# A hybrid encoder layer on one NeuronCore: the products and sums of its state space branch on VectorE, attention's tables through GpSimd's queue, one transfer where there were four

## The chip, the core and the metric

The kernel runs on one NeuronCore of a Trainium2 chip. The engines that appear below are TensorE (PE in the rows, and PEld for its weight loads), VectorE (DVE), ScalarE (ACT), GpSimd (POOL) and SyncE (SP), whose queue issues most of the transfers. The metric is device time in microseconds (us), the median of the runs: the kernel before takes 1432.58 us (three runs, 1430.61 to 1438.53).

## The reference

One layer of an encoder on 1024 tokens (a grid of 16 rows by 64 columns) of width 1024, all in float32. Three branches read the same projection and are merged through gates; a feed-forward part follows.

```python
h = rms_norm(x, g_mix);  z = h @ w_in          # Fourier 256 | q, k, v 3 x 512 | S5 input 256 | gates 3 x 1024
A = real(fftn(positions, group channels))      # 4 groups of 64 channels
B = neighbourhood_attention(q, k, v, rpb)      # 8 heads of 64, window 8 rows x 16 columns, a bias per head
# C: 16 groups of 16 channels, 64 complex states, both directions
lam_bar = exp(lam * dt);  bu = einsum('bsgc,gpc->bsgp', u, b_bar)
xs = associative_scan(x[t] = lam_bar * x[t-1] + bu[t])         # forward, and reversed
y = d_skip * u + sum over directions of real(einsum('bsgp,gcp->bsgc', xs, c))
y = gelu(y);  C = y * sigmoid(y @ w_glu)
merged = sum_i sigmoid(gate_i) * (branch_i @ w_br_i);  x = x + merged @ w_out
x = x + relu(rms_norm(x) @ w_up)**2 @ w_down;  out = rms_norm(x)
```

## The kernel before, in words

Activations lie transposed, channels on the 128 partitions, in two halves of 512 tokens. A float32 product is made of three matmuls on values split into a high and a low part: ScalarE writes the high part (`split`, line 196; `w_cut`, line 142) and VectorE subtracts it for the low one (lines 197, 143). The long projections run in `mm_main`, whose matmuls are line 171; they are called the main matmuls here, and every third of them makes a tick.

At each tick the branches, written as Python generators, may go on by a step. A branch has a rate (0.4 steps a tick for the state space branch, 0.57 for attention, 0.5 for the Fourier branch), and each `yield` in it ends a step. So a `yield` more puts what follows it behind two or three more ticks of main matmuls, and TensorE's instructions, in program order, are main matmuls with the branches' small ones between them. The other engines get their instructions in the order in which the Tile scheduler, with a timeline of its own, puts them; an engine works through its order and waits at an instruction whose inputs are not there.

The state space branch (`ssm`) treats its 16 groups in four quarters of four groups. `ssm_params` makes the exponentials and the powers pa, and bhat and bbar. Then three generators take turns. `ssm_prep` makes a quarter's matrices: `product` multiplies complex numbers of shape 128 x 512 into AA and BB, with some of the six multiplications and sums on GpSimd (G) and the rest on VectorE (V); line 464 transposes BB on TensorE, line 465 copies the result to BT on ScalarE; lines 454 and 455 put bbar into bz on GpSimd; line 469 multiplies bz by AA; kp and M come from that, M through eight transfers. `ssm_data` multiplies BT by U (line 501), turns the result by E (505 to 511), runs four scans on VectorE (515, 517), turns back (523 to 530), multiplies with M and AA (line 535) and writes Y to the scratch y_scr with four transfers. `ssm_gelu` reads yT back for every two quarters, once it is written, and computes GELU: Square on ScalarE (line 555), a product on VectorE (557), Tanh on ScalarE (559), a product on VectorE (561). At the end comes the GLU, whose weights glw are loaded at line 599.

Attention (`attn_pair`) runs over four pairs of heads, 16 units a pair: scores on TensorE (line 761), bias and maximum on VectorE (764, in the order's rows ISA), Exp on ScalarE (771), scaling by the reciprocal on VectorE or ScalarE (781, 779), transposes on TensorE (789), the split into p (196, 197), values on TensorE (806, 810), and the sum of two parts (819). Each unit loads a table bm of 192 KB four units ahead, and each two units a tile vj of 256 KB in four transfers of 64 KB out of the scratch v_scr. `attn_in` prepares q and k of the next pair (lines 722 to 730).

The first 40 us normalise the input, 40 to 100 us compute v, and up to 680 us run the gates' logits, the four pairs, the state space branch and the Fourier branch's start beside one another. After that come the merge (683 to 817 us) and the feed-forward part, where lines 165 and 1379 work.

Tiles come from pools with a set number of buffers: 36 of 4 KB (s), 21 of 2 KB (m) and 8 banks of PSUM. Who takes a buffer waits until its last reader is done.

## Time and profile before

| | |
|---|---|
| median of 3 runs | 1432.58 us (1430.61 to 1438.53) |
| profiled execution | 1433.98 us, of which the span of the trace is 1432.2 us |
| TensorE busy | 1383.5 us, 97% of the span |
| VectorE busy | 947.0 us |
| ScalarE busy | 572.0 us |
| GpSimd busy | 188.8 us |
| the chain that ended last | 83% of the span on TensorE, 7% on VectorE, 2% on transfers |

A row of a timeline gives the start, the duration, the engine, the line of the kernel, the operation with what it writes and reads, and in brackets how long the engine had been idle and who ended that. Consecutive instructions of an engine overlap a little at their ends, so the distance between two starts is what an instruction costs its engine. A row of the view by stretches gives each engine's busy time in a stretch, and behind that the mean clock that TensorE was granted (1.00 is 2.4 GHz, 0.50 is 1.2 GHz).

### The profile page before, as it was taken

The page shows a single profiled execution, that of the slowest core. Times are in us where ns is not written, and L with a number is a line of the kernel's source. Part 1 is how long each engine was busy: PE and PEld are TensorE (multiplying, and loading weights), DVE is VectorE, ACT ScalarE, POOL GpSimd, SP SyncE. Part 2 cuts the span into 40 slices and gives each one's busy share as a digit, 9 for nine tenths or more (in the row PEclk, how much of TensorE's full clock was granted, in tenths as well). Part 3 has the DMA queues.
Part 4 walks back from the last instruction along what each step waited for, and adds up shares of the span by engine and source line. Part 5 has one row for each costly group of instructions (what it writes and reads, how often), then busy time and mean ns, then how long its engine had stood idle before and what let it go on. Part 6 is the DMA issues. An engine that isn't in the chain of part 4 may idle for free.

```text
span 1432.2 us, 18648 instructions
## 1 busy us (share of the span) xinstructions
PE 1383.5 (97%) x6520; PEld 1152.1 (80%) x6520; DVE 947.0 (66%) x1764; ACT 572.0 (40%) x1087; POOL 188.8 (13%) x313
## 2 busy tenths in 40 slices
PE   6999988999999999999999999999999999999997
PEld 5778877788888888888788878888888788888885
DVE  6759876576473312543524797777777999878766
ACT  5512264566562211032401674333323364444244
POOL 3758611000000000000000003112211100000000
PEclk9999999999999999999999999999999999999998
DMA  6332453737563217411343226444447885454303
GB/s 227 136 121 82 132 165 99 215 111 239 170 215 127 99 42 255 145 43 35 96 162 114 78 89 213 140 154 148 143 155 265 278 298 176 147 175 143 96 8 117
DMA packets 110926, 209.62 MB, mean 146 GB/s; under 512 B 13681, under 2 KB 46833, under 8 KB 110833
## 3 DMA queue, kind: packets, MB, share of 16 engines
q1 hardware_dynamic: 100160, 174.09, 37.6%
q0 software_dynamic: 10672, 34.35, 6.5%
q8 instruction: 51, 0.84, 0.2%
q14 instruction: 43, 0.34, 0.1%
HBM read 146.52 MB, written 56.62 MB: 142 GB/s over the span
## 4 chain that ended last, share of the span: by engine, by line
PE 83%; DVE 7%; DMA 2%; issue 2%; ACT 1%; POOL 1%; SPq 1%; DVEq 0%; ACTq 0%; POOLq 0%
PE ps L165 45%; PE ps L171 34%; PE ps L789 1%; PE ps L806 1%; PE ps L810 1%; SPq L111 1%; DVE z L515 1%; DVE z L517 1%; DVE wl L143 0%; DMA vj<-v_scr 0%; PE ps L1083 0%; DMA bm<-in_rpb 0%; DVE BB L431 0%; DMA wr<-in_w_in 0%; DVE sm L764 0%
## 5 line engine op out<-in xcount | busy, mean ns | idle before, releaser
L165 PE MATMUL ps<-dw,dh 128*128 128x512 f32 x1344 | 306.1, 389 | 2.3 <-DVE dw L197 2.3
L165 PE MATMUL ps<-fb,uw 128*128 128x512 f32 x1344 | 306.6, 389 | 1.4 <-DVE t L1142 1.0
L165 PEld LDWEIGHTS ps<-dw,dh 128*128 128x128 f32 x1344 | 252.0, 188 | 55.7 <-DVE dw L197 3.2
L165 PEld LDWEIGHTS ps<-fb,uw 128*128 128x128 f32 x1344 | 251.9, 188 | 54.5 <-PE ps L1083 1.2
L171 PE MATMUL ps<-hTh,wh 128*128 128x512 f32 x576 | 231.7, 403 | 6.3 <-DVE mx L764 2.0
L171 PE MATMUL ps<-hTl,wh 128*128 128x512 f32 x576 | 227.6, 395 | 1.1 <-DVE hTl L200 1.1
L171 PE MATMUL ps<-hTh,wl 128*128 128x512 f32 x576 | 226.9, 394 | 0.0
L171 PEld LDWEIGHTS ps<-hTh,wh 128*128 128x128 f32 x576 | 109.3, 190 | 28.0 <-ACT wh L142 2.4
L171 PEld LDWEIGHTS ps<-hTh,wl 128*128 128x128 f32 x576 | 109.0, 189 | 22.9
L171 PEld LDWEIGHTS ps<-hTl,wh 128*128 128x128 f32 x576 | 109.5, 190 | 21.2 <-DVE hTl L200 1.5
L143 DVE TENSOR_TENSOR wl<-wr,wh 128x1024 fp32r<-128x1024 f32 (+2 forms) x76 | 72.5, 966 | 55.3 <-ACT wh L142 52.3
L196 ACT CAST dh<-da 128x512 fp32r<-128x512 f32 x112 | 69.5, 620 | 95.4 <-PE ps L165 61.2
L1379 DVE TENSOR_TENSOR x<-x,ps 128x512 f32<-128x512 f32 x112 | 73.6, 684 | 34.4 <-PE ps L165 34.3
L1295 POOL DMA_DIRECT2D h_scr<-hx x48 | 26.0, 541 | 493.7 <-ACT hx L1265 376.1
L197 DVE TENSOR_TENSOR dh<-da,dh 128x512 fp32r<-128x512 f32 x112 | 77.1, 688 | 13.8 <-ACT dh L196 13.8
L171 PE MATMUL ps<-act,wh 128*128 128x512 f32 x256 | 78.7, 390 | 0.1
L142 ACT CAST wh<-wr 128x1024 fp32r<-128x1024 f32 (+2 forms) x76 | 60.7, 821 | 32.1 <-PE ps L171 7.7
L196 ACT CAST uw<-us 128x512 fp32r<-128x512 f32 x64 | 38.1, 626 | 84.2 <-DVE us L1222 84.2
L1017 ACT ACTIVATE tg<-ps 128x512 f32<-128x512 f32 x32 | 19.1, 597 | 124.0 <-PE ps L171 118.6
L1267 DVE SCALAR_TENSOR_TENSOR hx<-hx 128x512 f32<-128x512 f32 x52 | 35.8, 689 | 40.7 <-ACT hx L1259 40.3
L764 DVE CUSTOM_DVE_ANT_0 sm<-ps,bm 128x384 f32<-128x384 f32 x64 | 35.3, 553 | 34.2 <-PE ps L165 24.2
L196 ACT CAST dw<-wd 128x512 fp32r<-128x512 f32 x80 | 49.4, 618 | 19.1 <-PE ps L165 18.4
(286 smaller groups left out, 2116.6 us busy)
## 6 DMA issues: line engine op xcount, KB each, us to landing
da<-h_scr SPq DMA_DIRECT2D x112, 256.0 KB
wr<-in_w_in SPq DMA_DIRECT2D x36, 512.0 KB
wu<-in_w_up SPq DMA_DIRECT2D x32, 512.0 KB
h_scr<-hs POOLq DMA_DIRECT2D x64, 256.0 KB, 2.6
wd<-in_w_down SPq DMA_DIRECT2D x64, 256.0 KB
bm<-in_rpb SPq DMA_DIRECT2D x64, 192.0 KB
h_scr<-hx POOLq DMA_DIRECT2D x48, 256.0 KB, 2.8
vj<-v_scr SPq DMA_DIRECT2D x128, 64.0 KB
```

The lines of the kernel that those rows point to most:

```text
L111: return self.nc.sync.dma_start(out=out, in_=in_)
L142: self.nc.scalar.copy(hi, r)
L143: self.nc.vector.tensor_tensor(out=lo, in0=r, in1=hi.bitcast(F32), op=ALU.subtract)
L165: self.nc.tensor.matmul(out=out, lhsT=l, rhs=r, start=start and i == 0, stop=stop and i == last, skip_group_check=more)
L171: self.nc.tensor.matmul(out=out, lhsT=l, rhs=r, start=i == 0, stop=i == last)
L196: nc.scalar.copy(hi, src)
L197: nc.vector.tensor_tensor(out=lo, in0=src, in1=hi.bitcast(F32), op=ALU.subtract)
L764: V.tensor_tensor_reduce(out=sm, in0=ps[:, 0:384], in1=bm.pop(u), scale=-1.0, scalar=3.0e38, op0=ALU.add, op1=ALU.min, accum_out=mx)
L1017: A.activation(tg, ps, AF.Tanh, scale=0.5)
L1267: V.scalar_tensor_tensor(out=x, in0=x, scalar=0.0, in1=x, op0=ALU.max, op1=ALU.mult)
L1295: self.nc.gpsimd.dma_start(out=self.t.h_scr[c, j - 1], in_=x)
L1379: self.nc.vector.tensor_tensor(out=self.x1[t][:, cs], in0=self.x1[t][:, cs], in1=self.banks[j][q], op=ALU.add)
```

## The change

On VectorE and GpSimd: all six operations of `product`, the product rz, and the sums and products of `ssm_data` are now on VectorE; `product` uses one temporary tile fewer, and the turn back uses the tiles of the turn again. The steps are cut differently: in `ssm_data` there is one more `yield` in the turn, one more between the two scans of each pair, and in the turn back the instructions stand two a step. The copies into bz are on ScalarE. Before quarter 0's transposes there are six empty steps in place of five.

Transfers: v_scr and y_scr are laid out so that one transfer loads a whole tile vj (32 of 256 KB in place of 128 of 64 KB) and one writes a quarter's Y. The loads of vj and bm are issued by GpSimd in place of SyncE. Channels of the branch are in another order, and the weights w_br_ssm and w_glu are permuted to suit on the host.

GELU and GLU: six empty steps stand between the load of yT and its Square, and glw is loaded when the second half's GELU begins, which is before the GLU starts.

```diff
...
-        self.y_scr = self.nc.dram_tensor("y_scr", (16, 16, 8, 128), F32, kind="Internal").ap()
+        self.y_scr = self.nc.dram_tensor("y_scr", (2, 8, 16, 8, 128), F32, kind="Internal").ap()
...
-        self.v_scr = self.nc.dram_tensor("v_scr", (1024, 1024), F32, kind="Internal").ap()
+        self.v_scr = self.nc.dram_tensor("v_scr", (4, W, 8, 4, P), F32, kind="Internal").ap()
...
         def product(out, x, y, sh):
...
-            t, u = self.m(sh, F32, "pt"), self.m(sh, F32, "pt")
-            G.tensor_tensor(out=t, in0=x[1], in1=y[1], op=ALU.mult)
+            t = self.m(sh, F32, "pt")
+            V.tensor_tensor(out=t, in0=x[1], in1=y[1], op=ALU.mult)
             V.tensor_tensor(out=out[:, 0], in0=x[0], in1=y[0], op=ALU.mult)
-            V.tensor_tensor(out=u, in0=x[1], in1=y[0], op=ALU.mult)
             yield
-            G.tensor_tensor(out=out[:, 1], in0=x[0], in1=y[-1], op=ALU.mult)
             V.tensor_tensor(out=out[:, 0], in0=out[:, 0], in1=t, op=ALU.subtract)
+            V.tensor_tensor(out=t, in0=x[1], in1=y[0], op=ALU.mult)
             yield
-            G.tensor_tensor(out=out[:, 1], in0=out[:, 1], in1=u, op=ALU.subtract if len(y) == 3 else ALU.add)
+            V.tensor_tensor(out=out[:, 1], in0=x[0], in1=y[-1], op=ALU.mult)
+            V.tensor_tensor(out=out[:, 1], in0=out[:, 1], in1=t, op=ALU.subtract if len(y) == 3 else ALU.add)
...
         G.memset(bz, 0.0)
         for i in range(2):
-            G.tensor_copy(bz[0:64, i, :, 0:16], bbar[0:64, i, gs, :])
-            G.tensor_copy(bz[64:128, i, :, 32:48], bbar[64:128, i, gs, :])
-        yield
-        for _ in range(5 if q == 0 else 0):
+            A.copy(bz[0:64, i, :, 0:16], bbar[0:64, i, gs, :])
+            A.copy(bz[64:128, i, :, 32:48], bbar[64:128, i, gs, :])
+        yield
+        for _ in range(6 if q == 0 else 0):
             yield
         BT = self.s([P, 4, 2, P], F32, "BT")
         for b in range(2):
...
-        G.tensor_tensor(out=rz, in0=self.ssm_keep[:, 0, 4 * q:4 * q + 4].unsqueeze(2).to_broadcast(sh),
+        V.tensor_tensor(out=rz, in0=self.ssm_keep[:, 0, 4 * q:4 * q + 4].unsqueeze(2).to_broadcast(sh),
                         in1=self.kmask.unsqueeze(1).to_broadcast(sh), op=ALU.mult)
         pv = []
         for i in range(2):
...
         V.tensor_tensor(out=tb, in0=pv[1], in1=E[:, 1], op=ALU.mult)
-        G.tensor_tensor(out=ta, in0=ta, in1=tb, op=ALU.add)
         yield
         V.tensor_tensor(out=tc_, in0=pv[1], in1=E[:, 0], op=ALU.mult)
         V.tensor_tensor(out=td, in0=pv[0], in1=E[:, 1], op=ALU.mult)
-        G.tensor_tensor(out=tc_, in0=tc_, in1=td, op=ALU.subtract)
+        yield
+        V.tensor_tensor(out=ta, in0=ta, in1=tb, op=ALU.add)
+        V.tensor_tensor(out=tc_, in0=tc_, in1=td, op=ALU.subtract)
         yield
         zs = [self.m(sh, F32, "z") for _ in range(2)]
         for v, z in ((ta, zs[0]), (tc_, zs[1])):
             V.tensor_tensor_scan(out=flat(z)[0:64, 1:L], data0=flat(rz)[0:64, 0:L - 1], data1=flat(v)[0:64, 0:L - 1],
                                  initial=0.0, op0=ALU.mult, op1=ALU.add)
+            V.memset(z[0:64, :, 0], 0.0)
+            yield
             V.tensor_tensor_scan(out=flat(z)[64:128, 0:L - 1][:, ::-1], data0=flat(rz)[64:128, 1:L][:, ::-1],
                                  data1=flat(v)[64:128, 1:L][:, ::-1], initial=0.0, op0=ALU.mult, op1=ALU.add)
-            V.memset(z[0:64, :, 0], 0.0)
             V.memset(z[64:128, :, NK - 1], 0.0)
             yield
-        ta, tb, tc_, td = (self.m(sh, F32, "v") for _ in range(4))
-        G.tensor_tensor(out=ta, in0=zs[0], in1=E[:, 0], op=ALU.mult)
+        V.tensor_tensor(out=ta, in0=zs[0], in1=E[:, 0], op=ALU.mult)
         V.tensor_tensor(out=tb, in0=zs[1], in1=E[:, 1], op=ALU.mult)
+        yield
         V.tensor_tensor(out=td, in0=zs[1], in1=E[:, 0], op=ALU.mult)
-        yield
-        G.tensor_tensor(out=tc_, in0=zs[0], in1=E[:, 1], op=ALU.mult)
+        V.tensor_tensor(out=tc_, in0=zs[0], in1=E[:, 1], op=ALU.mult)
+        yield
         V.tensor_tensor(out=ta, in0=ta, in1=tb, op=ALU.subtract)
-        yield
-        G.tensor_tensor(out=tc_, in0=tc_, in1=td, op=ALU.add)
+        V.tensor_tensor(out=tc_, in0=tc_, in1=td, op=ALU.add)
         yield
         yield
         ps = self.ps(sh)
...
         yield
-        for j in range(4):
-            self.dma(self.y_scr[4 * q + j].rearrange("c s k -> s c k"), Y[:, j, :])
+        self.dma(self.y_scr[q // 2, :, :, q % 2 * 4:q % 2 * 4 + 4].rearrange("s c g k -> (s c) g k"), Y)
         self.y_done += 1
...
             yield
-        self.tc.keep_in_program_order(self.dma(yT, self.y_scr[8 * hf:8 * hf + 8].rearrange("g c s k -> (g c) s k")))
+        self.tc.keep_in_program_order(self.dma(yT, self.y_scr[hf].rearrange("s c g k -> (c g) s k")))
+        for _ in range(6):
+            yield
         t1, g2 = self.s([P, 8, NK], F32, "t1"), self.s([P, 8, NK], F32, "g2")
         yield
         A.activation(t1, yT, AF.Square)
...
+        glw = []
+
         def after():
             for hf in range(2):
                 while self.y_done < 2 * hf + 2:
                     yield
+                if hf == 1:
+                    glw.append(self.m([P, 2, 2, P], F32, "glw"))
+                    self.dma(glw[0], self.a["w_glu"])
                 yield from self.ssm_gelu(hf)
...
             yield
...
         nc, V, A = self.nc, self.nc.vector, self.nc.scalar
-        wr = self.m([P, 2, 2, P], F32, "glw")
-        self.dma(wr, self.a["w_glu"])
         wh, wl = self.m([P, 2, 2, P], F32R, "glh"), self.m([P, 2, 2, P], F32R, "gll")
-        self.split(wh, wl, wr)
+        self.split(wh, wl, glw.pop())
...
             gh, gl = self.s([P, 1024], F32R, "gh"), self.s([P, 1024], F32R, "gl")
...
             t = self.m([P, 4, P], F32R, "vj")
-            c = pr * 256 + h * P
-            for r in range(4):
-                src = self.v_scr.rearrange("(g r c) x -> r c g x", r=4, c=W)[r, CS[j]:CS[j] + 32, :, c:c + P]
-                self.dma(t[32 * r:32 * r + 32].bitcast(F32), src)
+            src = self.v_scr[:, CS[j]:CS[j] + 32, 2 * pr + h].rearrange("r c g x -> r c (g x)")
+            G.dma_start(out=t.rearrange("p g x -> p (g x)").bitcast(F32), in_=src)
             vj[h, j] = t
...
         def bias(u):
             h, j, half = units[u]
             t = self.m([P, 384], F32, "bm")
-            self.dma(t, self.a["rpb"][2 * pr + h, half, JT[j]])
+            G.dma_start(out=t, in_=self.a["rpb"][2 * pr + h, half, JT[j]])
             bm[u] = t
...
-            self.dma(self.v_scr[t * P:(t + 1) * P, :], vt.rearrange("p h i c -> p (h i c)").bitcast(F32))
+            r = 2 * (t % 2)
+            self.dma(self.v_scr[r:r + 2, :, :, t // 2].rearrange("r c h x -> (r c) h x"),
+                     vt.rearrange("p h i c -> p h (i c)").bitcast(F32))
...
+    cg = np.arange(P).reshape(8, 16).T.reshape(P)
     for nm, kt in (("fn", 2), ("na", 4), ("ssm", 2)):
-        o["w_br_" + nm] = f["w_br_" + nm][0].reshape(kt, P, 8, P).transpose(2, 1, 0, 3)
+        w = f["w_br_" + nm][0].reshape(kt, P, 8, P)
+        o["w_br_" + nm] = (w[:, cg] if nm == "ssm" else w).transpose(2, 1, 0, 3)
...
-    o["w_glu"] = f["w_glu"][0].reshape(2, P, 2, P).transpose(1, 2, 0, 3)
+    o["w_glu"] = f["w_glu"][0].reshape(2, P, 2, P)[:, cg][..., cg].transpose(1, 2, 0, 3)
...
```

How that moves the engines' orders is seen at three places.

VectorE, matrices of quarter 0 (AA and BB are the matrices, pt the temporaries, tb and bhat what `ssm_params` still makes, vt the split of v). The first piece is before, the second the kernel as changed, with its own line numbers, in which `product` is lines 430 to 437.

```order
L432 TENSOR_TENSOR pt_786<-ssc_507,pa_746 128x512
L242 TENSOR_TENSOR tb_759<-ssb_505,pt_511 128x256
L243 TENSOR_TENSOR tb_759<-ssb_505,pt_511 128x256
L431 TENSOR_TENSOR BB_819<-bhat_751,pa_746 128x512
L244 TENSOR_TENSOR bhat_751<-tb_759 128x256
L435 TENSOR_TENSOR AA_784<-AA_784,pt_785 128x512
L197 TENSOR_TENSOR vt_811<-ps_775,vt_811 128x8x64
L432 TENSOR_TENSOR pt_821<-bhat_751,pa_746 128x512
L435 TENSOR_TENSOR BB_819<-BB_819,pt_820 128x512
L197 TENSOR_TENSOR vt_849<-ps_815,vt_849 128x8x64
```

```order
L431 TENSOR_TENSOR BB_818<-bhat_751,pa_746 128x512
L436 TENSOR_TENSOR BB_818<-bhat_751,pa_746 128x512
L433 TENSOR_TENSOR AA_784<-AA_784,pt_785 128x512
L197 TENSOR_TENSOR vt_810<-ps_775,vt_810 128x8x64
L244 TENSOR_TENSOR bhat_751<-tb_759 128x256
L434 TENSOR_TENSOR pt_785<-ssc_507,pa_746 128x512
L430 TENSOR_TENSOR pt_819<-bhat_751,pa_746 128x512
L437 TENSOR_TENSOR AA_784<-AA_784,pt_785 128x512
L433 TENSOR_TENSOR BB_818<-BB_818,pt_819 128x512
L197 TENSOR_TENSOR vt_847<-ps_814,vt_847 128x8x64
L434 TENSOR_TENSOR pt_819<-bhat_751,pa_746 128x512
L437 TENSOR_TENSOR BB_818<-BB_818,pt_819 128x512
```

In the changed kernel the last instruction of quarter 0's BB, the one of line 437, is VectorE's too, and AA and BB take twelve instructions of 128 x 512 on VectorE in place of six.

ScalarE, where the half's GELU begins (tg is a gate, t the GELU's tile with yT as input, BT the copy of the transposes, kp the matrix from which M is made). The first piece is before, the second and third the kernel as changed, where line 557 is the Square, 561 the Tanh, 821 the copy of attention's output and 774 its Exp.

```order
L727 CAST qk_1416<-ps_1500 64x512
L1042 ACTIVATE tg_1642<-ps_1572 128x512
L555 ACTIVATE t_287_1620<-yT_1535 128x1024
L465 COPY BT_1659<-ps_1660 128x512
L465 COPY BT_1659<-ps_1675 128x512
L559 ACTIVATE t_287_1620<-t_287_1620 128x1024
L473 COPY kp_1701<-ps_1692 16x4x128
L474 COPY kp_1701<-ps_1692 16x4x112
```

```order
L540 COPY Y_1578<-ps_1550 128x512
L454 COPY bz_1580<-bbar_750 64x4x16
L455 COPY bz_1580<-bbar_750 64x4x16
L454 COPY bz_1580<-bbar_750 64x4x16
L455 COPY bz_1580<-bbar_750 64x4x16
L465 COPY BT_1600<-ps_1601 128x512
L142 CAST wh_1658<-wr_1501 128x1024
L465 COPY BT_1600<-ps_1621 128x512
```

```order
L821 COPY ot_2123<-ps_2067 64x256
L196 CAST p_2026<-ps_2094 128x384
L196 CAST p_2061<-ps_2057 128x384
L782 ACTIVATE sm_1990<-sm_1990,rc_2048 128x384
L774 ACTIVATE sm_2091,su_2100<-sm_2091,mx_2092 128x384
L557 ACTIVATE t_402_2046<-yT_1627 128x1024
L782 ACTIVATE sm_2054<-sm_2054,rc_2120 128x384
L732 CAST qk_1970<-ps_1974 64x512
L732 CAST qk_1970<-ps_2116 64x512
L561 ACTIVATE t_402_2046<-t_402_2046 128x1024
```

Before, the Square of yT stands ahead of the two copies of BT; in the changed kernel it stands 48 rows behind the first of them, among attention's work of pair 0.

VectorE in attention pair 0 (z are the scans' results, v the turn's tiles, sm, mx, rc and p attention's tiles, qk the next pair's q). The first piece is before, the second the kernel as changed, where 516 and 520 are the scans, 728 the split of q, 767 bias and maximum, 780 and 784 the scaling.

```order
L819 TENSOR_TENSOR OT_1584<-ps_2013,ot_2084 64x16x16
L781 TENSOR_SCALAR sm_2047<-sm_2047,rc_2120 128x384
L764 ISA sm_2090,mx_2091<-ps_2087,bm_1941 128x384
L764 ISA mx_2091 128x1
L515 SCALAR_TENSOR_TENSOR z_2111<-rz_1887,v_1987 64x511
L517 SCALAR_TENSOR_TENSOR z_2111<-rz_1887,v_1987 64x511
L764 ISA sm_2126,mx_2127<-ps_2123,bm_1982 128x384
L764 ISA mx_2127 128x1
L197 TENSOR_TENSOR p_2008<-ps_2093,p_2007 128x384
L515 SCALAR_TENSOR_TENSOR z_2112<-rz_1887,v_1989 64x511
L517 SCALAR_TENSOR_TENSOR z_2112<-rz_1887,v_1989 64x511
L519 MEMSET z_2111 64x4
```

```order
L767 ISA mx_1816 128x1
L728 SCALAR_TENSOR_TENSOR qk_1662<-ps_1801,qk_1662 64x512
L767 ISA sm_1842,mx_1843<-ps_1839,bm_1725 128x384
L767 ISA mx_1843 128x1
L728 SCALAR_TENSOR_TENSOR qk_1663<-ps_1664,qk_1663 64x512
L197 TENSOR_TENSOR p_1877<-ps_1872,p_1876 128x384
L780 RECIPROCAL rc_1863<-su_1824 128x1
L728 SCALAR_TENSOR_TENSOR qk_1663<-ps_1801,qk_1663 64x512
L780 RECIPROCAL rc_1898<-su_1851 128x1
L767 ISA sm_1869,mx_1870<-ps_1866,bm_1766 128x384
L767 ISA mx_1870 128x1
L784 TENSOR_SCALAR sm_1815<-sm_1815,rc_1863 128x384
```

Before, four scans stand here in two pairs with attention's rows between; in the changed kernel two scans stand nine rows ahead of this piece, and between them and the scaling of the unit's sm in the last row come three splits of p, the first product of the turn back, four splits of q and three biases.

## Rows read from the trace of the kernel before

**Rows 1.** Page: busy time of each engine.

```profile
PE 1383.5 (97%) x6520; PEld 1152.1 (80%) x6520; DVE 947.0 (66%) x1764; ACT 572.0 (40%) x1087; POOL 188.8 (13%) x313
```

**Rows 2.** Busy time by stretch: engine, busy us (instructions), then clock, DMA.

```profile
78.00:90.00 12.00, 9.19 (x32) 7.05 (x30) 5.75 (x9) 1.66 (x3) 7.58 (x11) 0.72 0.43 175
165.00:190.00 25.00, 20.81 (x117) 17.22 (x116) 17.73 (x29) 8.73 (x17) 11.50 (x10) 1.00 0.60 184
190.00:242.00 52.00, 44.84 (x260) 38.55 (x259) 39.16 (x92) 28.68 (x66) 6.36 (x5) 0.93 0.44 120
250.00:306.00 56.00, 51.65 (x262) 42.91 (x261) 34.90 (x89) 34.92 (x77) 0.00 (x0) 0.97 0.49 149
306.00:680.00 374.00, 374.00 (x1858) 316.95 (x1857) 172.79 (x345) 129.95 (x266) 5.10 (x9) 1.00 0.44 140
```

**Rows 3.** TensorE's timeline, quarter 0's BB: start us, us, operation, [idle before].

```profile
79.31 0.39 PE L171 MATMUL ps<-wl,hTh 128*128 128x512 f32 x1
79.54 0.39 PE L171 MATMUL ps<-wh,hTl 128*128 128x512 f32 x1
82.01 0.30 PE L464 MATMUL ps<-konst,BB 128*128 128x128 f32 x1 [2.08 <-DVE BB L435]
83.04 0.90 PE L464 MATMUL ps<-konst,BB 128*128 128x128 f32 x3 [0.73 <-POOL BB L437]
```

**Rows 4.** Busy time by stretch, TensorE at half clock.

```profile
82.31:89.14 6.83, 6.10 (x18) 5.03 (x19) 1.44 (x3) 1.66 (x3) 3.20 (x7) 0.50 0.57 230
218.85:225.67 6.82, 5.64 (x13) 4.46 (x14) 6.49 (x23) 3.85 (x9) 3.31 (x3) 0.50 0.25 58
276.87:280.29 3.42, 3.42 (x14) 3.12 (x13) 1.55 (x7) 2.69 (x8) 0.00 (x0) 0.50 0.80 214
```

**Rows 5.** VectorE's timeline, chain of quarter 0.

```profile
69.63 0.68 DVE L431 TENSOR_TENSOR AA<-ssc,pa 128x512 f32<-128x512 f32 x1
70.23 1.28 DVE L239 TENSOR_TENSOR tb<-ssb,pt 128x256 f32<-128x256 f32 x1
```

**Rows 6.** GpSimd's timeline, last product of quarter 0.

```profile
81.28 1.71 POOL L437 TENSOR_TENSOR BB<-BB,pt 128x512 f32<-128x512 f32 x1
```

**Rows 7.** DMA issues of SyncE, yT.

```profile
174.49 0.43 SPq L111 DMA_DIRECT2D yT<-y_scr  x1
```

**Rows 8.** ScalarE's timeline, Square of yT.

```profile
180.00 1.06 ACT L555 ACTIVATE t<-yT 128x1024 f32<-128x1024 f32 x1 [12.08 <-DMA wr<-in_w_in]
```

**Rows 9.** TensorE's timeline, the wait behind it.

```profile
181.58 0.49 PE L165 MATMUL ps<-U,M 128*128 128x128 f32 x2 [1.96 <-ACT BT L465]
```

**Rows 10.** TensorE's timeline, waits of attention pairs 0 and 1, two undisturbed steps.

```profile
220.03 0.80 PE L171 MATMUL ps<-hTh,wh 128*128 128x512 f32 x1 [2.04 <-DVE mx L764]
...
276.54 0.62 PE L789 MATMUL ps<-konst,sm 128*128 128x128 f32 x3 [2.31 <-ACT sm L779]
...
288.50 0.72 PE L806 MATMUL ps<-p,vj 128*128 128x256 f32 x4
...
289.45 0.57 PE L165 MATMUL ps<-qk,qk 128*128 128x384 f32 x2
```

**Rows 11.** VectorE's timeline: scans beside GpSimd and alone, scaling of pair 0.

```profile
108.48 2.31 DVE L515 TENSOR_TENSOR_SCAN z<-rz,v 64x511 f32<-64x511 f32 x1
...
213.04 1.21 DVE L515 TENSOR_TENSOR_SCAN z<-rz,v 64x511 f32<-64x511 f32 x1
...
222.54 0.40 DVE L781 TENSOR_SCALAR sm<-sm,rc 128x384 f32<-128x384 f32 x1
```

**Rows 12.** VectorE's timeline, first and last of 16 scores of pair 1.

```profile
256.10 0.56 DVE L764 CUSTOM_DVE_ANT_0 sm<-ps,bm 128x384 f32<-128x384 f32 x1 [8.33 <-DMA t_scr<-tg]
...
299.83 0.54 DVE L764 CUSTOM_DVE_ANT_0 sm<-ps,bm 128x384 f32<-128x384 f32 x1
```

**Rows 13.** DMA issues: size, median us to landing.

```profile
h_scr<-hx POOLq DMA_DIRECT2D x48, 256.0 KB, 2.8
...
pt<-in_dft_p POOLq DMA_DIRECT2D x8, 512.0 KB, 4.7
```

## The prediction

> **What bounds the kernel now.** First the page's totals: TensorE is busy 1383.5 us of the 1432.2 us span, 97% [rows 1], so the end can move only by what TensorE loses. Then busy time by stretch, to see where that is. From 306 to 680 us TensorE is busy all 374.00 us, though attention pairs 2 and 3 run there [rows 2]; behind 680 us the change touches nothing. What it can touch is lost in four places [rows 2]: 12.00 - 9.19 = 2.81 us at 78 to 90 us (A), 25.00 - 20.81 = 4.19 at 165 to 190 (B), 52.00 - 44.84 = 7.16 in pair 0 (C), 56.00 - 51.65 = 4.35 in pair 1 (D). Last the clock: after three of these waits TensorE works at a granted clock of 0.50, that is 1.2 in place of 2.4 GHz [rows 4]. Half of its busy time there is the price, 3.05, 2.82 and 1.71 us, which belong to A, C and D. So A is worth 5.9 us, B 4.2, C 10.0, D 6.1, together 26.2: more than that nobody can gain here.
>
> Then the timelines, for what ends each wait. A: TensorE is out of work at 79.93 (82.01 less 2.08), waits for VectorE's line 435 until 82.01 and, after one transpose, for GpSimd's line 437 until 83.04 [rows 3, 6]. B: ScalarE sits 12.08 us idle ahead of the Square of yT, which starts at 180.00; the row names a transfer of w_in, but the Square reads yT, issued at 174.49 [rows 7, 8]. The copies of BT stand behind it in ScalarE's order, and the matmul that wants one waits 1.96 us [rows 9]; the rest of B is the attention behind it. C and D: the longest are 2.04 us for a bias and 2.31 for a scaled tile, which VectorE and ScalarE deliver late [rows 10]. In these stretches VectorE has scans and GELU or GLU among attention's rows.
>
> **The change part by part.** *A, products on VectorE.* Beside GpSimd, a scan takes 2.31 us on VectorE; with GpSimd at rest it takes 1.21 [rows 11]. The chain of quarter 0 starts at 69.63 with a 128 x 512 product of 0.68, the next instruction 0.60 later, and that one, a 128 x 256 product beside GpSimd, takes 1.28 [rows 5]. From there to the end of BB the changed order has 14 instructions of 128 x 512 (two of them splits of v) and six of 128 x 256. At 0.60 the first cost 8.4 us. For the six the trace has a time only beside GpSimd; I take 0.3 each, half the larger shape's, 1.8 us, and 1.28 each, 7.7 us, as the other end. GpSimd keeps four products of bbar, which now can run before 69.63 as no AA stands ahead of them; they slow the small instructions there, and I give them 1 us. BB is ready at 69.63 + 8.4 + 1.8 + 1.0 = 80.8 us. The sixth empty step moves the transposes behind six more main matmuls in the program order; at 0.23 us each (79.31 to 79.54, rows 3) they keep TensorE at work until 79.93 + 1.4 = 81.3. So nothing waits, by a narrow 0.5 us. I leave 0.3 us: A goes from 5.9 to 0.3. By the other end BB is ready at 86.7 and A is 5.4 plus 3.05, worse than now by 2.6.
>
> *B, yT.* In the changed order the Square stands 48 rows behind BT's copies on ScalarE, in the middle of pair 0, while the load is issued earlier. Nobody waits for yT then. The six empty steps cost nothing, as the GELU is needed only for the GLU. B goes from 4.2 to 0. The copies into bz, now in front of BT's on ScalarE, are four short ones on an engine that stood idle 12.08 us at this place [rows 8].
>
> *C, VectorE's 48 more instructions.* Twelve a quarter move from GpSimd, to VectorE, where at 0.60 they take 7.2 us a quarter, 28.8 in all. In pair 0 VectorE is busy 39.16 of 52 us [rows 2], so a quarter's 7.2 fit into the idle 12.8, and scans there already run at 1.21 since GpSimd has little left. What counts is the order. Behind the two scans and the splits of p, the changed order has, ahead of the scaling of the next unit's sm: one product (0.68), four splits of q (I take 0.68 each, as many columns as the product), three biases (0.56, rows 12), one split of p (0.56, as the bias) and the scaling itself (0.40, rows 11), with 0.3 for the tiny ones: 6.3 us. TensorE has meanwhile a step of values, 0.95 us (288.50 to 289.45), and one of scores, 0.35 [rows 10]. So it waits about 5.0 us for this one sm, and as after the waits of 2.04 and 2.31 [rows 10] the clock falls after it: 2.8 us as in rows 4. The later scans stand singly between attention's rows and cost little. I take 8 for C in place of 10. Bounds: 0, if VectorE runs ahead of its order's place by 6 us, since attention's start lies earlier by B; and 10.0 + 7.2 = 17, if a quarter's instructions are all paid.
>
> *D, GLU and glw.* The main matmuls ahead of the GLU go from some 760 to some 900 in the program order, so it leaves pair 1 and enters pair 2, where today's TensorE waits for nothing [rows 2]; quarter 3's turn and scans take its place in pair 1. I take half, 3 of 6.1; bounds 1 and 8. Into pair 2 I put 1 us, and 1 for a new tight place: quarter 1's BB, now VectorE's alone, stands close ahead of the transposes that want it, and is late by whatever VectorE is.
>
> *Transfers.* 128 issues of vj become 32 and y_scr's 16 become 4, and SyncE is rid of bm's 64: its queue is shorter, but nobody on the chain waits for it outside B, so this is nothing. GpSimd's queue takes 96 issues, in order. In front of them stand its last bbar products and memsets only; behind them the tables of the Fourier branch, needed much later. Transfers on that queue land 2.8 us after issue at 256 KB and 4.7 at 512 KB [rows 13]. A bm is loaded four units ahead; 15 units lie between 256.10 and 299.83 [rows 12], 2.9 us each, so the lead is 11.7 us. This hides them. If it doesn't, see the last rival.
>
> **Sum.** 26.2 now; afterwards 0.3 + 0 + 8 + 3 + 2 = 13.3. That is 12.9 us less. The profiled execution took 1433.98, 1.4 above the median of 1432.58; it would take 1421.1, the median 1419.7. I predict 1420.
>
> **Rivals.** *The stalls only move.* A and B go (9.8), but pair 0 pays a quarter's 7.2 us, with C and D otherwise as now: 1432.58 - 9.8 + 7.2 = 1430. For it speaks that VectorE becomes the one engine on which scans, products and attention queue; against it, the idle 12.8 us there. *The stalls go.* VectorE, free of GpSimd, runs ahead of its place and C and D end at 3 us together: 26.2 - 3 = 23 less, 1409. The undisturbed pairs 2 and 3 speak for it, the crowded order in pair 0 against. *GpSimd's queue is late*, on the slower side. Should an issue there wait for a buffer of the pool of 21, all tables behind it wait too, and with landing beyond the 11.7 us of lead the scores stall. It decides from that point on. One late table a pair costs up to its landing, 4.7, and the clock, 2.8: four pairs make 30, so 1420 + 30 = 1450. Against it: the pool frees a buffer with every unit, and the same transfers had the same lead on SyncE. The Trainium skill, in "SBUF — State Buffer", section "SBUF: two separate sides", has a rule for this side: transfers issued from GpSimd have their descriptors written by GpSimd's cores, which are locked out while VectorE runs a mode with both port pairs, as plain copies in float32 do. By it each table might start late by one such VectorE instruction, which the lead would hide unless many follow one another. The trace before has no table on this queue beside attention, so no row here shows it.
>
> **Chances.** Forecast 0.58 (its own range 1412 to 1428), stalls move 0.25, stalls go 0.07, queue late 0.10. A difference of 0.5%, 7.2 us, is about what a measurement tells from no change: faster is below 1425.4, slower above 1439.7. The forecast gives 0.53 to faster and 0.05 to same; the moving stalls 0.03, 0.19 and 0.03 (the spread about 1430); the vanishing ones 0.07 to faster; the queue 0.01 to same, 0.09 to slower. Faster 0.63, same 0.25, slower 0.12. The range of 8 in 10 is 1410 to 1434: it leaves out the best and the queue, and takes in most of the moving stalls.
>
> **What would show it.** A: the transposes of quarter 0 start without a wait near 81.3 us and the clock stays at 1.00 there. B: no idle of ScalarE ahead of the Square, no wait for BT. C: one wait of some 5 us at the transposes of a middle unit of pair 0, with 0.50 behind it; if it is absent, the time is nearer 1409. D: GLU's matmuls in pair 2. The queue: vj and bm land within 5 us, and no wait of VectorE's bias for bm. Wrong would be any loss behind 306 us over 3 us, or VectorE's split and scaling waiting for tables.

## The result, and the profile after

The changed kernel takes 1415.6 us, the median of four runs (1414.48 to 1417.07), against 1432.65 before. The ratio, reckoned from all the executions and not from the two medians, is 0.9875, 95% interval 0.9844 to 0.9906. The profiled execution took 1414.49, its span is 1412.7.

Busy time by stretch of the changed kernel, the same stretches as in [rows 2]:

```profile
78.00:90.00 12.00, 12.00 (x65) 9.81 (x65) 6.85 (x12) 2.50 (x5) 0.53 (x1) 1.00 0.61 177
165.00:190.00 25.00, 23.93 (x131) 19.91 (x129) 16.55 (x42) 13.38 (x29) 4.46 (x7) 1.00 0.48 138
190.00:242.00 52.00, 50.56 (x276) 43.81 (x277) 46.36 (x96) 28.48 (x61) 10.78 (x18) 0.93 0.56 163
250.00:306.00 56.00, 56.00 (x311) 48.32 (x310) 38.91 (x89) 38.08 (x80) 13.85 (x23) 1.00 0.72 202
306.00:680.00 374.00, 370.55 (x1824) 312.19 (x1822) 171.91 (x337) 126.66 (x261) 24.73 (x42) 1.00 0.39 125
```

Places A (78 to 90) and D (250 to 306) lose nothing in this execution. B and C together, 165 to 242, lose 25.00 - 23.93 and 52.00 - 50.56, that is 2.5 us in place of 11.35. From 306 to 680, where nothing was lost, it is 3.45, of which 1.60 are waits of the main matmuls that stood behind 680 us before and come earlier with everything else.

TensorE's waits in pairs 0 and 2, and then the stretches at half clock as in [rows 4]:

```profile
190.03 0.55 PE L792 MATMUL ps<-konst,sm 128*128 128x128 f32 x3 [1.10 <-DVE mx L767]
191.39 1.20 PE L809 MATMUL ps<-p,vj 128*128 128x256 f32 x4 [0.81 <-ACT sm L774]
...
194.67 0.87 PE L792 MATMUL ps<-konst,sm 128*128 128x128 f32 x3 [0.59 <-DVE sm L784]
...
341.48 0.39 PE L809 MATMUL ps<-p,vj 128*128 128x256 f32 x1 [1.57 <-ACT p L196]
```

```profile
37.41:40.83 3.42, 3.42 (x10) 2.65 (x9) 3.42 (x8) 3.39 (x5) 2.58 (x10) 0.50 0.01 2
...
191.01:197.84 6.83, 5.86 (x19) 4.89 (x20) 6.20 (x14) 3.60 (x10) 1.79 (x3) 0.50 0.32 97
```

The three waits at 190 to 195 us are what is left of pair 0. They cost 2.5 us and a half clock of 6.83 us, whose busy 5.86 are worth 2.9. The half clock at 37.41 lies ahead of all that is changed; it costs half of 3.42, 1.7 us, and stands in some executions of the kernels here and not in others: in run 1 as well, but not in runs 2, 10 and 11, whose code is the same up to there.

Place A, VectorE's first and last product of quarter 0 and TensorE's transposes of BB:

```profile
71.63 0.68 DVE L431 TENSOR_TENSOR AA<-ssc,pa 128x512 f32<-128x512 f32 x1
...
81.70 0.69 DVE L437 TENSOR_TENSOR BB<-BB,pt 128x512 f32<-128x512 f32 x1
...
82.81 0.60 PE L464 MATMUL ps<-konst,BB 128*128 128x128 f32 x4
```

VectorE in the place of the three waits, scans, the first and last of four splits of q (line 728) and the scaling that TensorE waits for last (784):

```profile
183.90 1.21 DVE L516 TENSOR_TENSOR_SCAN z<-rz,v 64x511 f32<-64x511 f32 x1 [1.05 <-PE ps L792]
185.14 1.22 DVE L520 TENSOR_TENSOR_SCAN z<-rz,v 64x511 f32<-64x511 f32 x1
...
188.69 0.68 DVE L728 SCALAR_TENSOR_TENSOR qk<-ps,qk 64x512 fp32r<-64x512 f32 x1
...
192.70 0.69 DVE L728 SCALAR_TENSOR_TENSOR qk<-ps,qk 64x512 fp32r<-64x512 f32 x1
...
194.10 0.42 DVE L784 TENSOR_SCALAR sm<-sm,rc 128x384 f32<-128x384 f32 x1
```

Transfers of the two tables on GpSimd's queue, median us to landing at the end:

```profile
bm<-in_rpb POOLq DMA_DIRECT2D x64, 192.0 KB, 4.8
...
vj<-v_scr POOLq DMA_DIRECT2D x32, 256.0 KB, 6.5
```

They land later than the transfers in [rows 13], the longest bm after 12.6 us, but VectorE waits for a table once, 0.9 us. yT is issued at 182.10 in this execution, 7.6 us later than before [rows 7], and ScalarE reaches its Square at 210.39 without a wait.

### The profile page after: what moved, and what is told of

It reads as the page before. It is cut to its first block, busy times and chain, and to the rows that moved or that the text cites. A ratio compares the mean times of both kernels' runs of the same rounds, so it can differ in the third digit from the quotient of the medians.

```text
span 1412.7 us, 18521 instructions
## 1 busy us (share of the span) xinstructions
PE 1378.5 (98%) x6520; PEld 1150.1 (81%) x6520; DVE 952.8 (67%) x1812; ACT 577.0 (41%) x1103; POOL 166.8 (12%) x345
## 4 chain that ended last, share of the span: by engine, by line
PE 71%; issue 18%; POOL 5%; DVE 2%; DMA 2%; ACT 1%; SPq 0%; POOLq 0%; DVEq 0%
PE ps L171 42%; PE ps L165 25%; POOL h_scr L1300 4%; PE ps L792 1%; PE ps L809 1%; PE ps L813 1%; DMA ssv<-in_ssm_v 1%; DMA wr<-in_w_in 1%; SPq L111 0%; PE ps L1088 0%; DMA yT<-y_scr 0%; POOL pt L249 0%; DMA h_scr<-hs 0%; PE ps L464 0%; POOL pt L250 0%
## 5 line engine op out<-in xcount | busy, mean ns | idle before, releaser
L171 PEld LDWEIGHTS ps<-act,wh 128*128 128x128 f32 x256 | 47.7, 188 | 10.0 <-ACT wh L142 0.5
```

Of the source, the lines that this page charges most:

```text
L171: self.nc.tensor.matmul(out=out, lhsT=l, rhs=r, start=i == 0, stop=i == last)
```

## The experiments

Each run gives a median and the ratio to the kernel before on the same chip, reckoned in the same way. Two theories stood at first: the gain comes from VectorE and the queues, or from the steps, that is from where in the engines' orders the branch's work stands.

**1. Tables on SyncE's queue**, from the changed kernel.

```diff
-            G.dma_start(out=t.rearrange("p g x -> p (g x)").bitcast(F32), in_=src)
+            self.dma(t.rearrange("p g x -> p (g x)").bitcast(F32), src)
-            G.dma_start(out=t, in_=self.a["rpb"][2 * pr + h, half, JT[j]])
+            self.dma(t, self.a["rpb"][2 * pr + h, half, JT[j]])
```

> The changed kernel, with the loads of vj and bm issued by SyncE again (one transfer a tile as in the changed kernel). Theory 1 (the queue is worth nothing; the gain comes from where instructions stand and from VectorE working without GpSimd): 1415 to 1418 us, pair 0's loss at 189 to 198 us as it is, no new wait of VectorE for bm. Theory 2 (the queue carries part of the gain, since SyncE's 128 + 64 issues held up yT and bm before): 1420 to 1426, with waits for bm or for transfers of q and k behind them.

1418.34 us, 0.9893 (0.9873 to 0.9912). This overlaps the changed kernel's interval: the medians lie 2.7 us apart, between the two theories, and what the queue is worth here may be nothing.

**2. No empty steps ahead of the Square**, from the changed kernel.

```diff
-        for _ in range(6):
-            yield
         t1, g2 = self.s([P, 8, NK], F32, "t1"), self.s([P, 8, NK], F32, "g2")
```

> The changed kernel without the six empty steps between the load of yT and its Square. The Square then stands 21 rows behind the last copy of BT on ScalarE, in place of 46. Theory 1 (it is enough that the Square stands behind BT's copies, the steps add nothing): 1415 to 1418 us. Theory 2 (the steps themselves carry place B's gain): ScalarE idles again ahead of the Square, attention's Exp waits behind it, 1419 to 1423.

1416.75 us, 0.9884 (0.9857 to 0.9910): theory 1 by the median, though the four executions spread from 1414.28 to 1420.87. In this order, with the sums' new steps, the Square stands behind BT without the empty ones.

**3. Sums on GpSimd again**, from the changed kernel: `product`, rz and the sums with `G` and `V` as before, 48 instructions.

```diff
-        V.tensor_tensor(out=rz, in0=self.ssm_keep[:, 0, 4 * q:4 * q + 4].unsqueeze(2).to_broadcast(sh),
+        G.tensor_tensor(out=rz, in0=self.ssm_keep[:, 0, 4 * q:4 * q + 4].unsqueeze(2).to_broadcast(sh),
...
-        V.tensor_tensor(out=ta, in0=ta, in1=tb, op=ALU.add)
+        G.tensor_tensor(out=ta, in0=ta, in1=tb, op=ALU.add)
```

> The changed kernel with product, rz and the state space sums on GpSimd where they were before (48 instructions), all else as changed: the steps, the copies of bz on ScalarE, the transfers on GpSimd's queue, behind these sums. Theory 1 (the gain of place A and part of C come from leaving GpSimd): the wait for BB and the half clock at 80 us return, 5.9 us, and scans of 2.3 us are back; 1421 to 1427 us. Theory 2 (the steps and the order carry it): 1415 to 1419. A third outcome, tables held up behind GpSimd's sums, would be above 1430.

1416.97 us, 0.9882 (0.9863 to 0.9902): theory 2. The medians lie 1.4 us apart, which the intervals do not tell from nothing. TensorE's waits for BB in this run:

```profile
82.59 0.30 PE L464 MATMUL ps<-konst,BB 128*128 128x128 f32 x1 [0.73 <-DVE BB L435]
83.63 0.55 PE L464 MATMUL ps<-konst,BB 128*128 128x128 f32 x3 [0.74 <-POOL BB L437]
```

They add up to 1.47 in place of 2.81 [rows 3], and no half clock follows. So most of what A lost comes back without VectorE's products; run 6, where the copies into bz are on GpSimd too, shows the same for the sixth empty step alone.

**4. Transfers alone**, on the kernel before: the layouts, `load_v`, `bias` and the single write of Y as in the diff.

> The kernel before with the transfers alone changed: the layouts of v_scr and y_scr, one transfer a tile vj and one a quarter's Y, vj and bm issued by GpSimd. Theory 1 (queue worth nothing but an earlier yT): place A and D stay, B loses some of its 4.2 us as yT is issued earlier; 1428 to 1433 us. Theory 2 (SyncE's long queue was what held attention's tables and yT): C and D shrink as well, 1420 to 1426. Tables late behind GpSimd's products: 1436 or more.

1443.78 us, 1.0081 (1.0051 to 1.0110): slower, as only the third outcome had it, but not for its reason. The chain in the timelines of SyncE, ScalarE, VectorE, GpSimd and TensorE, from cause to effect:

```profile
160.97 0.58 SPq L111 DMA_DIRECT2D y_scr<-Y  x1
...
169.92 0.37 SPq L111 DMA_DIRECT2D yT<-y_scr  x1
...
175.15 1.06 ACT L554 ACTIVATE t<-yT 128x1024 f32<-128x1024 f32 x1 [15.55 <-DMA qk<-qk]
...
176.23 1.22 DVE L556 SCALAR_TENSOR_TENSOR t<-t,yT 128x1024 f32<-128x1024 f32 x1 [14.76 <-ACT t L554]
...
178.22 1.22 DVE L515 TENSOR_TENSOR_SCAN z<-rz,v 64x511 f32<-64x511 f32 x1
...
181.00 2.22 POOL L523 TENSOR_TENSOR v<-z,E 128x512 f32<-128x512 f32 x1 [17.27 <-DVE z L520]
...
184.68 0.69 PE L165 MATMUL ps<-AA,bz 128*64 128x128 f32 x2 [13.87 <-POOL bz L455]
```

SyncE issues yT at 169.92, ScalarE reaches the Square at 175.15 after 15.55 us (the row names qk, but the Square reads yT), VectorE's line 556 stands ahead of the scans in its order, GpSimd's line 523 waits for the scans, bz stands behind it, and TensorE waits 13.87 us for bz. This is place B with a longer chain.

**5. The same with the six empty steps.**

```diff
+        for _ in range(6):
+            yield
```

> The kernel with the transfers alone changed (it took 1443.8), with the six empty steps ahead of the Square of yT as well. In that run TensorE waited 13.87 us for bz, behind GpSimd's line 523, behind VectorE's scans, behind VectorE's line 556 (the GELU's product), behind the Square of yT. Theory 1 (the place of the Square in the orders is the cause): the wait goes, 1426 to 1431 us, and this is also below the kernel before by place B. Theory 2 (GpSimd's queue holds up bz and the tables): 1440 or more.

1430.20 us, 0.9968 (0.9955 to 0.9981): 13.6 us back. TensorE's wait for bz is shorter and not gone, so theory 1 has the larger part of the cause and not all of it. SyncE, VectorE and TensorE:

```profile
161.69 1.38 SPq L111 DMA_DIRECT2D y_scr<-Y  x1
...
172.36 1.22 DVE L515 TENSOR_TENSOR_SCAN z<-rz,v 64x511 f32<-64x511 f32 x1 [7.51 <-DMA y_scr<-Y]
...
178.83 0.69 PE L165 MATMUL ps<-AA,bz 128*64 128x128 f32 x2 [5.95 <-POOL bz L455]
```

The scans, for which GpSimd's line 523 and behind it bz wait, start only when the write of quarter 1's Y has landed, 10.6 us after its issue. A scan does not read Y. Its z takes a buffer of the pool m, to which Y belongs, so by the rows this is a wait for a buffer; no run undoes it by itself.

**6. Steps alone**, on the kernel before: `ssm_data`'s steps, the order inside its turn back, its tiles, and 6 in place of 5; `G` and `V` as before.

```diff
+        yield
+        G.tensor_tensor(out=ta, in0=ta, in1=tb, op=ALU.add)
...
+            V.memset(z[0:64, :, 0], 0.0)
+            yield
```

> The kernel before with only the steps changed: three more steps a quarter in the state space sums (the turn, and between the two scans of each pair), the order inside the turn back, its tiles reused, and the sixth empty step of quarter 0. Engines and transfers as before. Theory P (steps carry the gain, by where they put the work and the GELU in the engines' orders): 1415 to 1421 us, no wait for BT, GLU in pair 2. Theory V (VectorE in place of GpSimd, or the transfers, are needed as well): 1424 or more.

1417.82 us, 0.9884 (0.9866 to 0.9901): theory P. The kernel before took 1434.01 on this chip, so with engines and transfers as they were 16 of the 17 us are there. Place A, which loses 1.53 at full clock, and pairs 0 and 1 of this run:

```profile
78.00:90.00 12.00, 10.47 (x57) 8.21 (x56) 6.66 (x10) 2.05 (x4) 6.62 (x10) 1.00 0.45 177
190.00:242.00 52.00, 48.29 (x259) 41.60 (x260) 43.05 (x91) 28.69 (x60) 8.94 (x7) 0.90 0.47 136
250.00:306.00 56.00, 56.00 (x317) 48.40 (x317) 40.50 (x90) 39.36 (x83) 0.00 (x0) 1.00 0.55 160
```

**7. All but the steps**, from the changed kernel: the old steps in `ssm_data`, 5 in place of 6.

> The changed kernel with the old steps in the state space sums and five empty steps in quarter 0; VectorE, the transfers, the six empty steps of the GELU and the early glw as changed. Theory P: most of the gain is lost, 1425 to 1432 us, though yT's Square still stands behind BT (so B stays gone, 4 us). Theory V: 1415 to 1420.

1431.87 us, 0.9992 (0.9979 to 1.0004): no change from before.

```profile
190.00:242.00 52.00, 43.36 (x222) 35.56 (x220) 42.85 (x99) 29.89 (x69) 11.39 (x19) 0.86 0.48 127
250.00:306.00 56.00, 55.99 (x299) 47.98 (x298) 37.03 (x94) 37.17 (x82) 12.46 (x22) 1.00 0.55 170
```

Pair 0 loses 8.6 us and 14% of the clock, although all 48 instructions are on VectorE. B did not stay gone, as theory P had it: the wait for BT is absent, but the stretch from 165 to 190 still loses 4.31 us, 3.10 of it for bz, again behind scans that start when the write of Y has landed: GpSimd's memset of bz waits for a product of VectorE (line 434) that stands behind them (VectorE, GpSimd, TensorE):

```profile
170.06 1.22 DVE L515 TENSOR_TENSOR_SCAN z<-rz,v 64x511 f32<-64x511 f32 x1 [3.72 <-DMA y_scr<-Y]
...
173.31 0.53 POOL L452 MEMSET bz<- 128x512 f32 x1 [14.09 <-DVE pt L434]
...
174.47 0.40 PE L165 MATMUL ps<-AA,bz 128*64 128x128 f32 x2 [3.10 <-POOL bz L452]
```

**8. Three empty steps** a quarter behind the scans, on the kernel before, and 6 in place of 5.

```diff
+        for _ in range(3):
+            yield
         ta, tb, tc_, td = (self.m(sh, F32, "v") for _ in range(4))
```

> The kernel before with three empty steps a quarter put behind the scans and the sixth empty step of quarter 0; nothing is cut finer and nothing else is changed. What comes after the scans then stands at the same main matmuls as with the steps of the changed kernel. Theory P1 (the place is what counts, for the GELU, the matrices that follow and the GLU): within 2 us of the run with the changed steps, 1416 to 1421. Theory P2 (the finer cut, one scan a step, is what counts, as it lets attention's short instructions in between): 1424 or more, with the waits of pair 0 behind pairs of scans.

1428.84 us, 0.9960 (0.9947 to 0.9972). By the expectation this speaks for the finer cut. The next run shows that it doesn't. Pair 0:

```profile
190.00:242.00 52.00, 43.63 (x229) 36.35 (x228) 35.90 (x83) 29.85 (x67) 5.96 (x4) 0.84 0.41 113
```

A further loss stands ahead of pair 0. GpSimd's order has the turn back of quarter 1 (line 525) behind quarter 2's BB, which starts after 13.73 us of idling, by the row for the transfers out of kp, and TensorE waits 2.57 us for the sums of the turn back (GpSimd, then TensorE):

```profile
154.64 1.50 POOL L434 TENSOR_TENSOR BB<-bhat,pa 128x512 f32<-128x512 f32 x1 [13.73 <-DMA M<-kp]
...
157.57 1.75 POOL L525 TENSOR_TENSOR v<-z,E 128x512 f32<-128x512 f32 x1
...
164.76 0.74 PE L165 MATMUL ps<-v,AA 128*128 128x128 f32 x2 [2.57 <-DVE v L530]
```

**9. Steps alone, scans paired again**, from run 6: both scans in one step, the next one empty.

```diff
-            V.memset(z[0:64, :, 0], 0.0)
-            yield
...
             V.memset(z[64:128, :, NK - 1], 0.0)
             yield
+            yield
```

> The run with the changed steps alone (1417.8), but both scans of a pair in one step again and the step behind them empty. The number of steps, and with it the place of all that follows, is the same; VectorE's order has the scans in the same rows, only their memsets move. Theory P (place): 1416 to 1420 us. Theory C (one scan a step lets attention's instructions in between): 1424 or more, with the empty steps behind the scans (1428.8) as its neighbour.

1418.18 us, 0.9884 (0.9865 to 0.9902), the same as run 6. So the cut between the scans is worth nothing here. Runs 8 and 9 differ in where the three steps stand, that is in how many main matmuls lie ahead of each pair of scans, but also in the order inside the turn back and in its tiles, which run 8 takes anew. Run 7 reuses the tiles and gains nothing, so the tiles alone do not do it; run 9 against run 8 does not separate the place from the order. Runs 10 and 11 move the place by itself.

**10 and 11. One step less, one step more** ahead of the scans, from the changed kernel.

```diff
         V.tensor_tensor(out=td, in0=pv[0], in1=E[:, 1], op=ALU.mult)
-        yield
```

```diff
+        yield
         zs = [self.m(sh, F32, "z") for _ in range(2)]
```

> The changed kernel with one step less in each quarter's turn, so that the scans and all behind them come one step earlier a quarter, some 7 main matmuls, and quarter 2's scans leave the splits of q in pair 0. Theory P: the loss of pair 0 at 188 to 198 us moves or changes by several us either way; 1411 to 1424 us, and GELU closer to BT again. Theory C (steps as such, fewer are worse): 1418 to 1424, by about a third of what the three steps brought.

> The changed kernel with one empty step more ahead of the scans of each quarter. Theory P: again a change of several us in pair 0 either way, and GLU still later, in pair 2 or behind it; 1411 to 1424 us. Theory C: no change from 1415.6, within 2 us, as nothing is cut finer.

One step less: 1409.15 us, 0.9828 (0.9806 to 0.9851), faster than both kernels. One step more: 1428.53, 0.9959 (0.9943 to 0.9975), with all of the change in place. Both are theory P, and both lie outside its 1411 to 1424. A step each way moves the time by 6 and by 13 us. Pairs 0 and 1 with one step more, and then with one less:

```profile
190.00:242.00 52.00, 44.10 (x233) 36.58 (x233) 38.95 (x86) 27.84 (x59) 9.92 (x17) 0.90 0.47 127
250.00:306.00 56.00, 56.00 (x319) 48.40 (x319) 40.59 (x102) 35.92 (x81) 16.16 (x27) 1.00 0.74 173
```

```profile
190.00:242.00 52.00, 48.58 (x270) 42.93 (x271) 42.03 (x88) 30.42 (x65) 8.47 (x14) 0.93 0.52 139
250.00:306.00 56.00, 56.00 (x307) 48.13 (x305) 40.39 (x91) 39.05 (x81) 13.12 (x22) 1.00 0.70 192
306.00:680.00 374.00, 372.34 (x1832) 313.91 (x1832) 171.46 (x343) 128.03 (x265) 26.00 (x44) 1.00 0.39 127
```

With one more, 7.9 us of pair 0 are lost. The profiled execution with one less is the slowest of its four runs, 1414.02 against 1408.56 to 1409.46. What it loses in pair 0 is one wait (ScalarE's split of q, then TensorE's transposes):

```profile
191.68 0.59 ACT L726 ACTIVATE qk<-ps 64x512 fp32r<-64x512 f32 x1 [6.87 <-DMA M<-kp]
...
193.42 0.90 PE L791 MATMUL ps<-konst,sm 128*128 128x128 f32 x3 [4.79 <-ACT sm L781]
```

The row names the transfers of M out of kp as what ended ScalarE's 6.87 us. Whether the other three executions lacked this wait, no trace shows. Place A is the same code as in the changed kernel, and here, without the half clock at 37 us, TensorE waits for it:

```profile
82.71 0.55 PE L464 MATMUL ps<-konst,BB 128*128 128x128 f32 x3 [0.96 <-DVE BB L437]
```

**12. The steps of that fastest run alone**, on the kernel before.

> The kernel before with the steps of the fastest run alone (one step more between the scans of each pair, none more in the turn, the order inside the turn back, the sixth empty step of quarter 0); engines and transfers as before. Theory P (place alone): it gains like the fastest run, 1409 to 1415 us, and is below the run with three steps a quarter (1417.8). Theory PV (the right place is worth this much only with VectorE and the shorter queue): 1418 to 1426.

1419.24 us, 0.9906 (0.9889 to 0.9922): theory PV. These steps need the rest of the change for 10 us. Its first wait in pair 0, in the timelines of SyncE, VectorE, ScalarE and TensorE:

```profile
166.19 1.85 SPq L111 DMA_DIRECT2D bm<-in_rpb  x4
...
178.61 0.34 SPq L111 DMA_DIRECT2D t_scr<-tg  x1
179.12 0.34 SPq L111 DMA_DIRECT2D yT<-y_scr  x1
...
183.15 0.56 DVE L764 CUSTOM_DVE_ANT_0 sm<-ps,bm 128x384 f32<-128x384 f32 x1 [3.40 <-DMA t_scr<-tg]
...
184.27 1.06 ACT L555 ACTIVATE t<-yT 128x1024 f32<-128x1024 f32 x1 [5.18 <-DMA yT<-y_scr]
...
183.77 0.89 PE L789 MATMUL ps<-konst,sm 128*128 128x128 f32 x3 [2.43 <-DVE mx L764]
```

VectorE's bias, the fourth of the pair, idles until 183.15. Its table was among the four issued at 166.19, and its scores were done at 181.35. The row names the transfer of tg to t_scr, issued at 178.61: the bias writes sm, which takes a buffer of the pool m, to which tg belongs, so by the rows it waits for a buffer. And the Square, with eight instructions between it and BT's second copy, holds ScalarE for 5.18 us. The six empty steps would take the second away; whether a shorter queue of SyncE would free the buffer sooner, no run shows, and neither was undone by itself at these steps.

Medians by the steps added a quarter and the rest of the change (the kernel before took 1432.65 to 1434.85 on the chips of these runs; the first row has five empty steps in quarter 0, the others six):

| steps | rest as before | rest as changed |
|---|---|---|
| none | 1432.65 | 1431.87 |
| two | 1419.24 | 1409.15 |
| three, as in the change | 1417.82 | 1415.60 |
| four | not run | 1428.53 |

## Why the prediction was right, and where its terms were off

The time, 1415.6, lies in the range and in the forecast's own range, and a gain of 17 us was forecast as 12.9. The four places were right, and what is left in them by the terms below is 5.4 and 1.85 us, together 7.25 in place of 13.3: C and D were taken too large. The terms:

- A: 0.3 us were left by the prediction, none in the trace, and this is partly luck. BB was ready at 82.39 and not at 80.8, as its chain began at 71.63 and not at 69.63 (the chain itself took 10.8 us, the sum 11.2). That TensorE was not out of work by then goes with the half clock at 37.41, which had cost it 1.7 us; with the same code and no such half clock it waits 0.94, 0.96 and 0.93 us (runs 2, 10, 11). The cause was shared differently from the way it was put: with VectorE alone and five empty steps (run 7) TensorE still waited 0.64 and 1.53 us for BB, with a half clock behind; with the sixth step alone (run 6) it lost 1.53 and kept its clock. So the step is worth about 4.3 of the 5.9 us and VectorE about 0.6, and the prediction had told of the engines first.
- B: gone, as forecast, but not all by the way that was put. The load of yT was not issued earlier, it was issued 7.6 us later. That the Square's place in the order holds up what stands behind it is shown by runs 4 and 5. But with the Square behind BT and the old steps the stretch still loses 5.95 and 4.31 us (runs 5 and 7), most of it behind the write of Y, while with the steps alone nothing waits for BT (run 6): it was the steps that took B away. That the six empty steps cost nothing holds, but here they also bring nothing clear of the noise (run 2).
- C: forecast 8, measured 2.5 + 2.9 = 5.4. The place was right: from the memsets behind the scans, 187.9, to the end of the scaling at 194.52 VectorE takes 6.6 us, and the sum said 6.3. But the one wait of some 5 us for this scaling came as 0.59; two others, 1.10 and 0.81, stand ahead of it. The term that was mis-sized is TensorE's cover: 1.3 us were counted, but TensorE waited only 2.5 of the 6.6, so it had 4.1 us of work of its own, as it also had the transposes of the unit before and did part of it at half clock.
- D: forecast 3 in pair 1 and 2 elsewhere, measured 0 and 1.85, of which 1.57 in pair 2 as said, where TensorE waits for ScalarE's split of p among GLU's matmuls. Halving D without a row was the largest error. With GLU gone from pair 1 all of D went (in run 7, where GLU starts at 305 us with the old steps, the stretch loses 0.01 us too), though no run moves GLU by itself. Quarter 3's scans did not take its place: they start at 232.41, ahead of the pair's first bias at 242.43.
- Queue: nothing clear of the noise (run 1), as forecast. The rival with late tables did not come: tables landed later than assumed, bm 4.8 and vj 6.5 us by the median (run 6, where SyncE issues them, has 3.7 for bm), and the longest bm, 12.6, went 0.9 over the lead of 11.7; the tables cost VectorE 0.9 us, once. The rule of the Trainium skill in "SBUF — State Buffer", section "SBUF: two separate sides", that transfers issued from GpSimd can start late beside VectorE's instructions in a mode with both port pairs, would fit the longer landing, but no run here separates it from the traffic of the other queues.
- VectorE's 48 instructions: the 7.2 us a quarter fit into its idle time, as argued. But so did GpSimd's way of doing them: 1.4 us lie between the two, inside the noise (run 3). The prediction gave the moved engine a part in A and the steps only a place in B and D; runs 6 and 7 show the steps carry nearly all at the changed kernel's steps, while at one step less (runs 10 and 12) the rest is worth 10 us.
- Its sign of being wrong, a loss of more than 3 us behind 306, came by the letter, 3.45; 1.60 of that had stood behind 680 before.

What stays open: why run 8 is 11 us slower than run 9 is seen in one wait, 2.57 us for the turn back, and in a larger loss of pair 0 (run 9 loses 4.9 there), which is not traced; what in the rest of the change is worth 10 us at two steps; and how much of run 10's gain is chance in M's transfers.

## What to carry to other kernels

If a bounding engine is fed by engines that work through fixed orders, the place of the side work's steps can be worth more than moving work between engines: here the steps alone gave 16 of 17 us, all the rest alone 1 or nothing, and one step more or less after that +13 or -6. The two are not a plain sum: with one step less the rest was worth 10 us. So when a change moves both, undo each by itself, and then try a step either way. And look in each engine's order for an instruction that waits for a transfer and stands ahead of work the bounding engine needs: its cost is its place.

## What had not been expected of the hardware

A wait named by a row was twice not the one that held the engine: at 180.00 [rows 8] and in run 4 the row named another transfer, and what the instruction reads told the truth. In runs 5, 7 and 12 the row named a transfer that the instruction does not read, and there it was the buffer that the instruction writes which told more: the transfer had to be done before a tile of the same pool came free. A half clock of 3.42 us came at 37.41 in this execution and not in runs 2, 10 and 11, though the code up to there is the same; it costs 1.7 us, of which some 0.9 come back at place A, where TensorE then has not to wait.
